# Window attention: the softmax rows scaled inside the transposing product, with a diagonal matrix as its second operand

## The chip, the cores and the metric

The kernel runs on one core of one Trainium2 chip. The metric is the device time of one execution in microseconds. A core has a matrix engine, TensorE (PE in the profile, with its weight loads shown apart as PEld), three engines that work on tiles, VectorE (DVE), ScalarE (ACT) and GpSimd (POOL), and SyncE (SP), whose queue issues most of the DMAs. Each engine runs its own instructions in a fixed order and waits on semaphores for the others. Products of TensorE land in PSUM; GpSimd works on tiles in SBUF only.

## The reference

Two layers work on 512 latent tokens and 256 context tokens of width 1024. Each layer is half a SwiGLU network, a token mixer, and another half SwiGLU network, each closed by a layer norm. The mixer of the second layer ("Mixer 1") is windowed attention with 16 query heads on 4 key heads of 64 columns: a block of 128 queries sees its own block of keys, the block on either side of it within a band, and all 256 context keys, and each head has one extra logit, the sink, which counts in the sum but has no value.

```
s_win  = where(valid, einsum('bqhgd,bkhd->bhgqk', qb, kb), NEG_INF)
s_ctx  = einsum('bqhgd,bkhd->bhgqk', qb, kc)
p = softmax(concatenate([s_win, s_ctx, s_sink], axis=-1))
o = einsum(p[..., :n_win], vb) + einsum(p[..., n_win:n_win + C], vc)
```

## The kernel before

The program is recorded in Python, and a scheduler fixes the order of the instructions on each engine from the dependencies and from its own table of costs; a helper (`behind`) pins a few orders by hand. Tokens lie along the free axis, features along the 128 partitions, and every large product is done in three products of split operands (`mm3`, L166, L168, L169). The weights come through `wunit`: SP loads four raw quarters `wr`, ACT casts each to `wh` (L105), and POOL subtracts to get the rest `wl` (L107). This splitting for later units goes on during the attention, on the same POOL queue that scales the softmax rows.

Mixer 1 is `wa_mixer`. It runs eight units of `attn(s, ...)`, each with two heads h (columns 0 to 63 and 64 to 127 of the partitions), and each over four blocks b of 128 queries. Between the units TensorE has other work: the query projections of a later unit (`wq`), the rotary product (`prq`, L1153), and the output projection of the two units before (`pow`, `wo_pairs`). For one block:

1. `scores` (L888, L889) writes the scores of each head to a PSUM bank, `sw`. Blocks 0 and 3 have two window blocks of keys and fit the context scores behind them, 512 columns. Blocks 1 and 2 have three, 384 columns, and the 256 context scores go to a bank of their own, `sc` (the program calls this `split`).
2. DVE adds the mask and takes the row minimum (L1244, L1247); scores are kept negative, so the minimum stands for the maximum.
3. ACT takes exponentials into SBUF tiles `pw` (L1259) and, for split blocks, `pc` (both heads side by side, L1261), with the row sums `l` and `lc`, and the sink's share `le` (L1263).
4. DVE adds the sums (L1269 or L1272) and takes the reciprocal, 1/l (L1273).
5. POOL multiplies each row of `pw`, and of `pc` for split blocks, by its 1/l in place (`scale_p`, L933).
6. TensorE transposes the tile by blocks of 128 columns against the identity `idn` into a PSUM bank `tpw` or `tpc` (`transpose`, L914). Blocks 0 and 3 have four such products for each head, blocks 1 and 2 have three of `pw` for each head and four of `pc` for both: over the eight units 224 of `pw` and 64 of `pc`.
7. ACT and DVE in turn copy the transposed tile back over the old one (`evac`, L861, L863).
8. TensorE multiplies the transposed tiles with the values `vtw` (`pv_mm`, L924) into the bank `wo`, both heads at a time, 224 and 64 products again. At the end of a unit `split_o` (L929, L930) takes the result out.

The PSUM banks set how far blocks overlap: two banks for `sw`, two for `sc` (shared with other uses), one with tag `t` and two with tag `mm` for the transposes. In the phase's pool, tag `v` has eight tiles of 256 columns in Mixer 1 (`vbufs[0] = 8`, L1135): six for the values, and the rest, with all eight later on, for the normalized inputs `ufl` of the network that follows (L322).

Mixer 0 has its own attention (`na_mixer`) with the same helpers `transpose` and `scale_p`.

## Time and profile before

| | us |
|---|---|
| median of 3 runs | 2696.71 |
| lowest, highest | 2695.93, 2699.86 |
| the profiled execution | 2694.58 |
| its span, first to last instruction | 2692.8 |
| TensorE busy | 2616.0 (97%) |
| VectorE busy | 1810.1 (67%) |
| GpSimd busy | 1676.2 (62%) |
| ScalarE busy | 1198.2 (44%) |
| attention of Mixer 1 in the span | about 2085 to 2305 |

A group row of the profile gives the source line, the engine, the operation, the tiles (out<-in), the shape, how many records there are, then the busy time and the mean duration of one, and then the idle time of the engine just before them with what ended it. A matmul's duration is its latency: the next one starts long before it ends, so the pace of a run of matmuls is read from the starts in the timeline. The chain of waits follows the end of the program back, step by step, to what released each instruction. A releaser such as "POOL pw L933" names the engine, the tile and the line.

### The profile page before, as it was taken

How to read it: one execution, taken by the hardware profiler on the slowest of the kernel's cores; microseconds unless marked ns; L12 is line 12 of the kernel's file. 1: busy time of each engine (PE TensorE's matmuls, PEld its weight loads, DVE VectorE, ACT ScalarE, POOL GpSimd, SP SyncE). 2: the span in 40 equal slices, each digit the busy share in tenths (PEclk: the TensorE clock that was granted, in tenths of full speed). 3: DMA queues.
4: the chain of work that ended last, by engine and by line, in shares of the span. 5: the costliest groups of instructions: out<-in, count | busy, mean ns of one | idle time of the engine just before them, and what ended most of it. 6: DMA issues, size and time to landing. Idle time of an engine off the chain costs nothing.

```text
span 2692.8 us, 47575 instructions
## 1 busy us (share of the span) xinstructions
PE 2616.0 (97%) x16826; PEld 2385.8 (89%) x16826; DVE 1810.1 (67%) x4269; ACT 1198.2 (44%) x2475; POOL 1676.2 (62%) x1523
## 2 busy tenths in 40 slices
PE   8999999999999999999999999999999999899997
PEld 5899999888988899999998899999988777899997
DVE  4977777775445686656565866666668776787765
ACT  5244343266455453443432534434336654544443
POOL 4786767455443566967664678676645544678773
PEclk9999999999999999999999999999999999999999
DMA  9367565523221122454453225546652111243332
GB/s 328 104 180 203 138 163 167 146 70 81 61 57 55 48 74 77 124 132 123 123 135 102 79 78 150 142 133 188 185 152 66 33 32 40 69 117 94 102 92 67
DMA packets 290574, 303.50 MB, mean 113 GB/s; under 512 B 27297, under 2 KB 192417, under 8 KB 289313
## 3 DMA queue, kind: packets, MB, share of 16 engines
q1 hardware_dynamic: 277952, 278.31, 35.1%
q0 software_dynamic: 12096, 22.03, 4.9%
q8 instruction: 133, 2.18, 0.3%
q14 instruction: 105, 0.85, 0.1%
q10 hardware_dynamic: 288, 0.14, 0.0%
HBM read 292.53 MB, written 12.25 MB: 113 GB/s over the span
## 4 chain that ended last, share of the span: by engine, by line
PE 84%; DVE 8%; ACT 3%; issue 2%; DMA 2%; POOL 2%; SPq 0%; POOLq 0%; DVEq 0%; ACTq 0%
PE pd1a L166 2%; PE pd0b L166 2%; PE pd1a L169 2%; PE pd1a L168 2%; PE pd0b L168 2%; PE pd0b L169 2%; PE pd0a L166 2%; PE pd0a L169 2%; PE pd0a L168 2%; PE pd1b L169 1%; PE pd1b L166 1%; PE pd1b L168 1%; DVE z L513 1%; PE wo L924 1%; PE o L924 1%
## 5 line engine op out<-in xcount | busy, mean ns | idle before, releaser
L107 POOL TENSOR_TENSOR wl<-wr,wh 128x512 fp32r<-128x512 f32 x200 | 261.9, 1326 | 163.9 <-ACT wh L105 94.4
L107 POOL TENSOR_TENSOR wl_s<-S,wh_s 128x512 fp32r<-128x512 f32 x240 | 314.3, 1342 | 45.9 <-ACT wh_s L105 29.1
L105 ACT CAST wh_s<-S 128x512 fp32r<-128x512 f32 x256 | 157.2, 621 | 398.7 <-POOL S L655 79.1
L655 POOL TENSOR_TENSOR S<-wr,wr 128x512 f32<-128x512 f32 x128 | 175.3, 1370 | 193.7 <-DMA wr<-in_wst_dram 162.3
L215 DVE CUSTOM_DVE_ANT_0 jk<-wt,cb 128x512 f32<-128x512 f32 x360 | 244.6, 680 | 22.3 <-DMA wt<-in_wmodt_dram 18.2
L107 POOL TENSOR_TENSOR wl_a<-wr,wh_a 128x512 fp32r<-128x512 f32 x144 | 190.7, 1372 | 17.1 <-ACT wh_a L105 13.1
L105 ACT CAST wh_a<-wr 128x512 fp32r<-128x512 f32 x192 | 119.0, 621 | 163.2 <-PE pd1b L168 29.9
L105 ACT CAST wh<-wr 128x512 fp32r<-128x512 f32 x200 | 121.2, 618 | 101.8 <-DMA wr<-in_wst_dram 18.3
L513 DVE SCALAR_TENSOR_TENSOR z<-pd0b,gt,z 128x256 f32<-128x256 f32 (+1 forms) x168 | 96.8, 595 | 43.5 <-PE pd0b L169 43.1
L513 DVE SCALAR_TENSOR_TENSOR z<-pd1a,gt,z 128x512 f32<-128x512 f32 (+1 forms) x150 | 88.2, 605 | 37.3 <-PE pd1a L169 37.1
L513 DVE SCALAR_TENSOR_TENSOR z<-pd0a,gt,z 128x512 f32<-128x512 f32 (+1 forms) x160 | 93.4, 612 | 15.3 <-PE pd0a L169 15.1
L933 POOL TENSOR_SCALAR p<-p,l 128x512 f32<-128x512 f32 x64 | 44.2, 694 | 84.6 <-DVE l L1047 79.8
L655 POOL TENSOR_TENSOR S<-wr,S 128x512 f32<-128x512 f32 x64 | 90.7, 1417 | 2.6
L655 POOL TENSOR_TENSOR S<-S,wr 128x512 f32<-128x512 f32 x64 | 90.6, 1415 | 1.8
L933 POOL TENSOR_SCALAR pw<-pw,l 128x512 f32<-128x512 f32 (+1 forms) x64 | 42.5, 666 | 69.3 <-DVE l L1273 39.7
L343 POOL TENSOR_SCALAR z<-z,ag_None,ab_None 128x256 f32<-128x256 f32 (+1 forms) x69 | 52.1, 759 | 53.3 <-DVE uh L328 34.7
L513 DVE SCALAR_TENSOR_TENSOR z<-pd1b,gt,z 128x512 f32<-128x512 f32 (+1 forms) x91 | 55.1, 622 | 25.3 <-PE pd1b L169 24.8
L1046 ACT ACTIVATE p<-s,m 128x512 f32<-128x512 f32 x64 | 43.8, 687 | 60.5 <-DVE m L1043 57.6
L329 DVE TENSOR_TENSOR ul<-ufl,uh 128x256 fp32r<-128x256 f32 (+1 forms) x88 | 59.1, 676 | 4.2 <-ACT ufl L322 1.9
L322 ACT ACTIVATE ufl<-z,bi_None,sc_None 128x256 f32<-128x256 f32 (+1 forms) x77 | 47.7, 637 | 30.8 <-DVE z L498 30.4
L107 DVE TENSOR_TENSOR wl_a<-wr,wh_a 128x512 fp32r<-128x512 f32 x48 | 58.9, 1236 | 1.6 <-ACT wh_a L105 1.5
L166 PE MATMUL vn<-wh,uh 128*128 128x256 f32 x192 | 54.5, 284 | 0.4 <-DVE nl L882 0.3
(1483 smaller groups left out, 10518.5 us busy)
## 6 DMA issues: line engine op xcount, KB each, us to landing
wr<-in_wst_dram SPq DMA_DIRECT2D x456, 256.0 KB
wt<-in_wmodt_dram SPq DMA_DIRECT2D x206, 256.0 KB
wr_0b<-in_wst_dram SPq DMA_DIRECT2D x47, 256.0 KB
wr_1b<-in_wst_dram SPq DMA_DIRECT2D x47, 256.0 KB
wr_2b<-in_wst_dram SPq DMA_DIRECT2D x47, 256.0 KB
wr_3b<-in_wst_dram SPq DMA_DIRECT2D x47, 256.0 KB
wm<-in_wmod_dram SPq DMA_DIRECT2D x8, 1024.0 KB
zspare<-in_wmodt_dram SPq DMA_DIRECT2D x30, 256.0 KB
```

The source lines that it names most:

```text
L105: nc.scalar.copy(hi[:], src[:])
L107: x = eng.tensor_tensor(out=lo[:], in0=src[:], in1=hi[:].bitcast(F32), op=ALU.subtract)
L166: behind(nc.tensor.matmul(ps, a[0], b[0], start=first, stop=False), in_front[0])
L168: nc.tensor.matmul(ps, a[0], b[1], start=False, stop=False)
L169: last_pe[0] = nc.tensor.matmul(ps, a[1], b[0], start=False, stop=last)
L215: x = nc.vector.tensor_tensor_reduce(out=junk[:], in0=w[:], in1=cb[st], scale=1.0, scalar=0.0, op0=ALU.mult, op1=ALU.add, accum_out=out[st])
L329: return hi, nc.vector.tensor_tensor(out=lo, in0=uv, in1=uo.bitcast(F32), op=ALU.subtract)
L343: nc.gpsimd.tensor_scalar(out=zs, in0=zs, scalar1=prm[2][:, d:d + 1], scalar2=prm[3][:, d:d + 1], op0=ALU.mult, op1=ALU.add)
L513: last[0] = nc.vector.scalar_tensor_tensor(out=zt(d, c0, c1), in0=pd, scalar=gt[:, d, st:st + 1], in1=zt(d, c0, c1), op0=ALU.mult, op1=ALU ...
L655: nc.gpsimd.tensor_tensor(out=t[:], in0=a[:], in1=b[:], op=o)
L924: last_pe[0] = nc.tensor.matmul(po[64 * h:64 * h + 64, :], t[h][0], t[h][1], start=i == 0, stop=i == len(terms) - 1)
L933: nc.gpsimd.tensor_scalar(out=p, in0=p, scalar1=r, scalar2=0.0, op0=ALU.mult, op1=ALU.add)
```

## The change

The row scaling moves from GpSimd into TensorE's transposing product. `transpose` gets a new argument `by`: without it (Mixer 0) it still transposes against the identity, with it each block is an ordinary matrix product of the tile with a diagonal matrix. The product of a tile's transpose with diag(1/l) is the transposed tile with each query's column scaled. `diagonal` makes that matrix on GpSimd, the identity times 1/l, 128 by 128, in one of two buffers with tag `dg`. One diagonal serves all blocks of a head, in `pw` and in `pc`. `vbufs[0]` in Mixer 1 goes from 8 to 7, which makes the room.

```diff
-    def transpose(nm, p, order, tags):
+    def transpose(nm, p, order, tags, by=None):
...
         for j, s in enumerate(order):
-            nc.tensor.transpose(pt[:, j * P:(j + 1) * P], p[:, s * P:(s + 1) * P], idn[:])
+            if by is None:
+                nc.tensor.transpose(pt[:, j * P:(j + 1) * P], p[:, s * P:(s + 1) * P], idn[:])
+            else:
+                nc.tensor.matmul(pt[:, j * P:(j + 1) * P], p[:, s * P:(s + 1) * P], by[s][:], start=True, stop=True)
...
+    def diagonal(nm, r):
+        t = ph["S"].tile([P, P], F32, tag="dg", name=f"dg{nm}", bufs=2)
+        nc.gpsimd.tensor_scalar(out=t[:], in0=idn[:], scalar1=r, scalar2=0.0, op0=ALU.mult, op1=ALU.add)
+        return t
...
-        vbufs[0] = 8
+        vbufs[0] = 7
...
-                es = []
+                es, dg = [], []
...
                     nc.vector.reciprocal(lh, lh)
-                    scale_p(es[h], lh)
-                    if split:
-                        scale_p(ec[:, h * 256:(h + 1) * 256], lh)
-                    transpose(f"w{nm}_{h}", es[h], range(es[h].shape[1] // P), tags)
+                    dg.append(diagonal(f"{nm}_{h}", lh))
+                    transpose(f"w{nm}_{h}", es[h], range(es[h].shape[1] // P), tags, [dg[h]] * 4)
...
                 if split:
-                    transpose(f"c{nm}", ec, range(4), tags)
+                    transpose(f"c{nm}", ec, range(4), tags, [dg[0], dg[0], dg[1], dg[1]])
```

The scheduler orders all engines of the attention anew. Line numbers from L914 on grow by 1 to 8. Tiles are named with the unit, the block and the head: `pw2_1_0` is unit 2, block 1, head 0; `pc2_1` holds both heads of that block; the last number only tells buffers apart.

GpSimd's queue at the beginning of unit 2, before:

```order
L107 TENSOR_TENSOR wl121_0_24594<-wr121_0_24591,wh121_0_24593 128x512
L933 TENSOR_SCALAR pw2_0_1_24049<-pw2_0_1_24049,l2_0_24029 128x512
L107 TENSOR_TENSOR wl121_1_24600<-wr121_1_24597,wh121_1_24599 128x512
L933 TENSOR_SCALAR pw2_1_0_24100<-pw2_1_0_24100,l2_1_24079 128x384
L933 TENSOR_SCALAR pc2_1_24099<-pc2_1_24099,l2_1_24079 128x256
L107 TENSOR_TENSOR wl121_2_24606<-wr121_2_24603,wh121_2_24605 128x512
L933 TENSOR_SCALAR pw2_1_1_24104<-pw2_1_1_24104,l2_1_24079 128x384
L933 TENSOR_SCALAR pc2_1_24099<-pc2_1_24099,l2_1_24079 128x256
L933 TENSOR_SCALAR pw2_2_0_24164<-pw2_2_0_24164,l2_2_24143 128x384
L933 TENSOR_SCALAR pc2_2_24163<-pc2_2_24163,l2_2_24143 128x256
L107 TENSOR_TENSOR wl121_3_24612<-wr121_3_24609,wh121_3_24611 128x512
```

And the same place with the change:

```order
L107 TENSOR_TENSOR wl121_0_24610<-wr121_0_24607,wh121_0_24609 128x512
L940 TENSOR_SCALAR dg2_0_1_24072<-idn_74,l2_0_24037 128x128
L107 TENSOR_TENSOR wl121_1_24616<-wr121_1_24613,wh121_1_24615 128x512
L940 TENSOR_SCALAR dg2_1_0_24120<-idn_74,l2_1_24089 128x128
L107 TENSOR_TENSOR wl121_2_24622<-wr121_2_24619,wh121_2_24621 128x512
L107 TENSOR_TENSOR wl121_3_24628<-wr121_3_24625,wh121_3_24627 128x512
L940 TENSOR_SCALAR dg2_1_1_24129<-idn_74,l2_1_24089 128x128
L940 TENSOR_SCALAR dg2_2_0_24184<-idn_74,l2_2_24153 128x128
```

The four scalings of block 1 have become two diagonals, and that of head 1 now stands behind both `wl121_2` and `wl121_3` instead of behind the first alone. In units 4 and 6 it stands the same way.

TensorE's queue at the end of unit 3, before (`wq2_0` is the query projection that follows; `tpw3_2_0` stands further up):

```order
L924 MATMUL wo3_0_24258<-pw3_1_0_24331,vtw_0_23036 64x128
L914 MATMUL tpc3_2_24421<-idn_74,pc3_2_24394 128x128 x2
L914 MATMUL tpw3_2_1_24416<-idn_74,pw3_2_1_24399 128x128 x3
L914 MATMUL tpc3_2_24421<-idn_74,pc3_2_24394 128x128 x2
L914 MATMUL tpw3_3_0_24464<-idn_74,pw3_3_0_24455 128x128 x4
L166 MATMUL wq2_0_24513<-uh0_101,wh120_0_24491 128x512
```

And with the change:

```order
L927 MATMUL wo3_0_24270<-pw3_1_0_24345,vtw_0_23036 64x128
L917 MATMUL tpw3_2_0_24421<-dg3_2_0_24419,pw3_2_0_24409 128x128 x3
L917 MATMUL tpc3_2_24435<-dg3_2_0_24419,pc3_2_24408 128x128 x2
L917 MATMUL tpc3_2_24435<-dg3_2_1_24428,pc3_2_24408 128x128 x2
L917 MATMUL tpw3_3_0_24479<-dg3_3_0_24477,pw3_3_0_24469 128x128 x4
L166 MATMUL wq2_0_24529<-uh0_101,wh120_0_24507 128x512
```

The number of products is the same; their second operand is now `dg`, whose two buffers alternate. `dg3_3_0` takes the buffer of `dg3_2_0`, so GpSimd can fill it only when the first pair of `tpc3_2` is done, and `tpw3_3_0` stands one pair behind that.

## The prediction

> **What bounds the kernel now.** I read the page first, then the stage by windows, then the chain of waits in it, and last single runs of matmuls in the timeline. The page's busy line says that TensorE carries the whole span:
>
> ```profile
> PE 2616.0 (97%) x16826; PEld 2385.8 (89%) x16826; DVE 1810.1 (67%) x4269; ACT 1198.2 (44%) x2475; POOL 1676.2 (62%) x1523
> ```
>
> An average over the span says little of 220 us of it, so the attention of Mixer 1 is read in windows (columns: busy us and records of PE, PEld, DVE, ACT, POOL, then the granted clock):
>
> ```profile
> 2085.00:2125.00 40.00, 35.31 (x288) 27.93 (x286) 30.55 (x118) 26.66 (x82) 19.61 (x28) 0.96 0.06 14
> 2125.00:2180.00 55.00, 52.79 (x386) 42.01 (x384) 37.28 (x117) 31.32 (x88) 24.06 (x32) 1.00 0.13 34
> 2180.00:2235.00 55.00, 51.23 (x370) 40.29 (x369) 39.36 (x122) 29.61 (x87) 25.66 (x33) 1.00 0.15 39
> 2235.00:2305.00 70.00, 60.15 (x432) 48.12 (x431) 52.20 (x162) 37.96 (x105) 35.89 (x44) 0.98 0.17 46
> sum 220.00, PE 199.49 PEld 158.35 DVE 159.40 ACT 125.55 POOL 105.23; mean PE 49.87 PEld 39.59 DVE 39.85 ACT 31.39 POOL 26.31
> ```
>
> TensorE is busy 91% of these 220 us and GpSimd 48%. In the middle, where projections fill in between units, TensorE stands still for only 2.2 and 3.8 us; at both ends the softmax of a block goes round DVE, ACT and POOL and TensorE waits. What it waits for (longest totals, weight loads and matmuls):
>
> ```profile
> PEld sw L888 <- ACT pw L1259: 14.9, 20, 2.1
> PEld tpw L914 <- POOL pw L933: 6.3, 15, 1.1
> PEld wo L924 <- DVE pw L863: 3.0, 7, 1.1
> PE tpw L914 <- POOL pw L933: 2.4, 6, 0.9
> ```
>
> The wait that ends last is mostly for an exponential to free a score bank. The scaling on POOL, which the change shortens, ends 6.3 us of waiting. The chain through this window, by line, is:
>
> ```profile
> by line: PE wo L924 13.6%; PE tpw L914 6.9%; DVE sw L1244 5.7%; PE sw L888 5.6%; issue 4.8%; PE wq L166 4.2%; PE wq L169 4.2%; PE wq L168 4.1%; ACT pw L1259 4.0%; PE pow L166 3.9%; PE sw L889 3.7%; PE pow L168 3.6%; PE pow L169 3.3%; DVE l
> ```
>
> The transposes themselves are second in it, with 6.9% of 220 us = 15.2 us for `tpw`; POOL's scaling is below the part of the line that the view shows.
>
> **What the change does to TensorE** is the main term. The diff replaces a transpose by a matrix product of two float32 tiles, the same number of times. These rows tell that the two are not the same on the engine:
>
> ```profile
> L914 PE MATMUL tpw<-idn,pw x224: 270/273/476, 2088.5 to 2299.4; 128*128 128x128 f32 x112
> L914 PE MATMUL tpc<-idn,pc x64: 270/273/332, 2094.9 to 2293.7; 128*128 128x128 f32 x64
> L924 PE MATMUL wo<-pw,vtw x448: 272/273/324, 2092.5 to 2301.3; 128*64 128x128 f32 x150
> L924 PE MATMUL wo<-pc,vtw x128: 272/273/324, 2098.1 to 2296.7; 128*64 128x128 f32 x128
> ```
>
> The program has 224 transposes of `pw` and 64 of `pc`, and the trace has one record for each. It has as many products with the values, and the trace has two records for each, 448 and 128: an ordinary float32 product runs as two matmuls, each with its own weight load, a transpose as one. The nearest product in size is the one of the layer norms that spreads a row (`spread`, L407): 128 by 128 against `idn`, float32, exactly the new shape. Beside a run of transposes from the timeline:
>
> ```profile
> 2021.36 1.13 PE L407 MATMUL prl<-idn,yl 128*128 128x128 f32 x8
> 2022.24 0.36 PE L166 MATMUL pd1a_l<-gh1a_l,wh_1b 128*128 128x256 f32 x1
> 2259.46 1.04 PE L914 MATMUL tpw<-idn,pw 128*128 128x128 f32 x8
> 2260.25 0.37 PE L888 MATMUL sc<-wk,wq 128*128 128x256 f32 x1
> ```
>
> Eight records of `prl` are four products (the call over 512 columns makes n // P of them); the next matmul starts 0.88 us after the first, 0.22 us for each product. Eight records of `tpw` are eight products, and the next starts after 0.79 us, 0.099 for each. So each of the 288 products costs about 0.12 us more, **34.6 us** of TensorE time in all.
>
> How much of it lies on the path? The chain holds 15.2 us of `tpw`. `tpc` is below the cut of that line; in proportion of the counts (64 to 224) it adds 4.3, together 19.5 us of 288 x 0.099 = 28.5, about two thirds. The products on the path get 2.2 times as long: 19.5 x 0.22 / 0.099 less 19.5 is +23.8 us if that path stays. Where another engine's wait is as long as the extra 0.3 to 0.5 us of one call, part of it hides; where it is shorter, part of the other third comes on the path. The ends are 0 (all of it in the 20.5 us in which TensorE is idle here, which is less than 34.6, so some 14 would remain even then) and 34.6. I take **+24**.
>
> **What it does to GpSimd.** These go, 96 instructions and 57.9 us:
>
> ```profile
> L933 POOL TENSOR_SCALAR pw<-pw,l 128x512 f32<-128x512 f32 x32 | 23.8, 745 | 30.4 <-DVE l L1273 20.3 <-PE wo L924 4.9 <-ACT wh L105 2.3
> L933 POOL TENSOR_SCALAR pw<-pw,l 128x384 f32<-128x384 f32 x32 | 18.8, 586 | 38.9 <-DVE l L1273 19.4 <-DVE l L1269 10.8 <-DVE l L1272 3.4
> L933 POOL TENSOR_SCALAR pc<-pc,l 128x256 f32<-128x256 f32 x32 | 15.3, 479 | 0.0
> ```
>
> In their place come 64 of 128x128, a shape the trace does not have. From 479 at 256 columns and 586 at 384, each 128 columns cost about 107 ns, so 372 at 128; it is below 479 in any case and, by half of it, above 240. That is 24 us, and 34 us of POOL's work vanish. POOL stood idle half the time, so what counts is the wait that its latency ends: the 6.3 us shrink with 372 against 586 to 745, by a third to a half. In split blocks the second head also no longer stands behind the `pc` of the first. Between 0 and the whole 6.3, I take **-3**.
>
> **The new waits.** A diagonal has two buffers, so the one of a later block waits on POOL until the products that read the buffer are through, and what stands behind it in that queue waits too. The place with the shortest distance is the end of units 3 and 5, where `tpw3_3_0` stands one pair of `tpc3_2` (0.44 us) behind the pair that frees its buffer, while the diagonal takes 0.37 and two hand-overs; some 0.3 us each. In units 2, 4 and 6 the diagonal of head 1 now follows two weight subtractions, of which one more than before is ahead of it:
>
> ```profile
> L107 POOL TENSOR_TENSOR wl<-wr,wh 128x512 fp32r<-128x512 f32 x29 | 37.8, 1308 | 21.7 <-ACT wh L105 19.6 <-PE wq L169 1.8
> ```
>
> That is 1.3 us three times at most, 3.9, if nothing covers it, and TensorE has other products there (the transposes of head 0, eight PV products). Range 0 to 5, I take **+1**.
>
> **What is moved or nearly free.** No DMA is added, and SP's queue keeps its order. POOL frees the raw quarters `wr` by its subtractions, and one such load stands in the chain:
>
> ```profile
> 2260.01 0.67 POOL pw L933
> 2260.68 1.25 POOL wl L107
> 2261.95 3.10 DMA wr<-in_wst_dram
> ```
>
> With 0.37 in place of 0.67 ahead of it the load starts 0.3 earlier; with a subtraction moved ahead of scalings, up to the whole 3.1. I take **-1**. The `v` buffers, seven for eight: the inputs `ufl` that use them are written by ACT in 0.6 us each and read by DVE at once, and DVE waited for one only 1.5 us in all (row below); three free buffers cover that, so nothing, 1.5 if they don't.
>
> ```profile
>   ACT ufl L322: 1.5, 1
> ```
>
> The scheduler's new order of the attention's queues I can only bound: no rule says that it is worse, and with the waits above of 1 or 2 us each, a few more or fewer make 4 us either way; taken as 0.
>
> **Clock.** Two stretches of the attention had a lower granted clock:
>
> ```profile
> 2085.00:2090.00 5.00, 2.72 (x11) 1.56 (x10) 4.09 (x19) 2.79 (x10) 1.37 (x2) 0.85 0.16 42
> 2090.00:2095.00 5.00, 4.93 (x39) 4.35 (x40) 4.00 (x19) 3.72 (x15) 1.95 (x4) 0.81 0.00 0
> 2285.00:2290.00 5.00, 3.21 (x14) 2.92 (x15) 3.39 (x18) 4.35 (x15) 1.69 (x3) 0.66 0.00 0
> ```
>
> 5 x (0.15 + 0.19 + 0.34) = 3.4 us of clock went in these. Both lie where TensorE idles (2.72 and 3.21 busy of 5), which the change does not cure, so 0; a gain of 3.4 at most. The Trainium skill, TensorE: Matmul & The Clock Gate, Part 4: PE-mode transpose, says that transposes do not count as busy for the clock gate. By that rule ordinary products in their place would keep the clock up, and these 3.4 us would come back; the idle in the same rows speaks for the simpler reason.
>
> **Sum.** 24 - 3 + 1 - 1 = **+21 us**. The profiled execution took 2694.58 us (span 2692.8), so 2715.6 beside it; the median of the three runs is 2.1 higher, and by that it is 2717.7. I forecast **2717 us**, 0.8% slower, with 2708 to 2726 as its own range (a third more or less of the main term is 8).
>
> **The rivals.** First, on the other side, **TensorE pays nothing**: the scaled product runs like a transpose, one record, and only POOL's relief counts. That gives -3 to -6.3 for the wait, up to -3.1 for the load: about 2690. For it speaks that a matmul's duration is 273 ns in both kinds of row; against it, that the records are counted double for every float32 product, `prl` among them. 5%. The same skill section puts a transpose at about 275 ns in a kernel's context, and FP8 and Floating Point Precision, section Matmul Precision, a true float32 product at four passes; as an estimate from these pages at 2.4 GHz that is 4 x 128 columns = 213 ns, less than 275, and the change would give back 288 x 0.062 = 18 us, 2679; of the 5% I give it one. The rows differ from the first: transposes start every 0.099 us here, and 273 is only their latency; they agree with the second, at 0.22.
>
> Second, **the waits swallow it**: the extra 0.3 to 0.5 us of a call falls into the 14.9 us of waiting for exponentials, POOL's gains come on top, and the sum is 34.6 - 20.5 - 8, about +6 or less: 2697 to 2705. For it: the ends of the stage are loose, 4.7 and 9.9 us idle. Against it: the transposes are on the path there themselves, ahead of the PV products and of the bank. 14%.
>
> Third, **all of it is exposed, and the new waits too**: 34.6 + 5 - 3, 2733. For it: the middle of the stage has almost no idle time, and the single bank with tag `t` holds back the next transpose longer. Against it: a third of the transposes were off the path. 16%.
>
> **Chances.** The forecast 62%; it pays nothing 5%, the waits swallow it 14%, all exposed 16%; the rest, 3%, is a better order of the queues. The range 2701 to 2733 leaves out the first rival, the lower half of the second and a tail above. A measurement of this kernel can tell about 0.2%, 5.4 us, from no change, so "same" reaches to 2702. Faster 0.05 (the first rival alone), same 0.09 (most of the second), slower 0.86.
>
> **What would show it.** TensorE with 288 records more, 17114, `tpw` with 448 and `tpc` with 128 at a pace of 0.11 us; 64 diagonals on POOL near 372 ns, and POOL's total down by some 34 us; the stage about 241 us long; `tpw` and `tpc` with some 40 us in its chain; little wait behind POOL. Wrong would be a count of 16826, or a stage of unchanged length with the idle time of TensorE gone from its ends.

## The result

The changed kernel took 2715.57 us in the median of 17 runs (2708.79 to 2723.88), the kernel before, in 17 runs beside it, 2700.22. The ratio is 1.0053, 95% interval 1.0041 to 1.0065: **14.3 us slower**, 11 to 17.5. The forecast of 2717 us came close, and part of that is luck: it had 21 us of loss, two thirds of which came, and the kernel before took 3.5 us more in these runs than in the three that the 21 were added to. The single runs of one kernel spread by some 15 us, in part with their granted clock: of the changed kernel's, the seven below 2712 us had 0.995 or 0.996 of it, the ten above 0.992 to 0.996.

The busy line of the page of the profiled execution (2711.55 us, span 2709.7) with the change:

```profile
PE 2643.1 (98%) x17114; PEld 2422.4 (89%) x17114; DVE 1815.7 (67%) x4269; ACT 1199.0 (44%) x2475; POOL 1647.9 (61%) x1491
```

There are 288 more records on TensorE and its busy time is 27.1 us longer, while GpSimd lost 28.3 us and 32 instructions. The four windows of the attention, with the columns of the prediction's fence:

```profile
2085.00:2125.00 40.00, 36.69 (x326) 32.16 (x326) 31.94 (x118) 25.49 (x80) 7.49 (x17) 1.00 0.03 10
2125.00:2180.00 55.00, 54.21 (x421) 46.47 (x421) 33.70 (x112) 30.11 (x85) 17.51 (x25) 1.00 0.14 40
2180.00:2235.00 55.00, 54.72 (x410) 46.12 (x411) 37.52 (x120) 30.47 (x86) 18.68 (x24) 1.00 0.13 39
2235.00:2305.00 70.00, 66.93 (x493) 56.96 (x492) 43.95 (x127) 32.36 (x90) 23.85 (x30) 1.00 0.13 39
```

TensorE is now busy nearly all of the time even in the last window (66.93 of 70, before 60.15), and GpSimd, the fifth busy time of a row, does a half to two thirds of what it did. Equal windows hold different work, though, since the changed kernel is later and later. So from here on the **stage** is measured from the first score product (`sw`) to the first product of the next network (`pa1b`), and read as one window. Before:

```profile
2083.90:2309.00 225.10, 203.56 (x1501) 162.16 (x1499) 163.81 (x530) 128.47 (x368) 109.23 (x140) 0.98 0.14 38
```

With the change:

```profile
2084.90:2325.90 241.00, 229.29 (x1790) 195.82 (x1788) 162.55 (x530) 129.60 (x368) 77.61 (x108) 1.00 0.12 35
```

The stage grew from 225.1 to 241.0 us, by 15.9. (The forecast's 241 was 220 plus 21, in windows that begin later and end earlier; that both read 241 is chance.) Busy time of TensorE grew by 25.7, its idle time fell from 21.5 to 11.7 us, by 9.8; busy and idle time make up the stage, so this is bookkeeping and not yet a cause. What follows the stage is as long as before, 369.6 against 369.4 us to the end of the last matmul. GpSimd did 31.6 us less in the stage; what that was worth is asked below. Every stage length here is read from the one profiled execution of its kernel. The clock in it falls to half in stretches of 3.4 us, which cost up to 1.7 us each: there were two in this stage before and none with the change, so a difference of 2 us between two kernels can be one such stretch.

The groups by tile show what the 288 records are (columns: count, then shortest, median and longest duration in ns, first and last start):

```profile
L917 PEld LDWEIGHTS tpw<-dg,pw x448: 186/192/193, 2089.2 to 2316.2; 128*128 128x128 f32 x150
L917 PE MATMUL tpw<-dg,pw x448: 270/275/377, 2089.4 to 2316.3; 128*128 128x128 f32 x150
L917 PE MATMUL tpc<-dg,pc x128: 270/275/377, 2095.1 to 2310.5; 128*128 128x128 f32 x128
L940 POOL TENSOR_SCALAR dg<-idn,l x64: 367/373/787, 2088.7 to 2312.2; 128x128 f32<-128x128 f32 x64
```

448 for 224 and 128 for 64; the duration of one record hardly moved (275 ns for 273). The pace is in the timeline, at the place that the prediction showed:

```profile
2263.82 1.16 PE L917 MATMUL tpw<-dg,pw 128*128 128x128 f32 x8
2264.74 0.36 PE L888 MATMUL sw<-wk,wq 128*128 128x256 f32 x1
```

Eight records are now four products in 0.92 us, 0.23 for each. The chain through the stage names them first:

```profile
by line: PE tpw L917 19.6%; PE wo L927 14.4%; PE tpc L917 6.2%; PE sw L888 5.4%; PE pow L166 5.3%; PE pow L168 4.9%; PE pow L169 4.7%; PE sw L889 4.6%; PE wq L166 3.8%; PE wq L168 3.8%; PE wq L169 3.8%; DVE sw L1252 2.6%; PE prq L1161 2.0%;
```

25.8% of 241 is 62 us, where `tpw` alone had 15.2 before. All 288 products together take 68.2 us (worked out below), so about nine tenths of them are on the path. And the waits:

```profile
PEld sw L888 <- ACT pw L1267: 4.7, 8, 2.1
PEld tpw L917 <- POOL dg L940: 4.3, 8, 1.3
POOL dg L940 <- DVE l L1281: 30.2, 22, 4.4
POOL dg L940 <- PE tpc L917: 21.0, 6, 4.6
POOL dg L940 <- PE tpw L917: 13.3, 8, 2.9
```

The wait for an exponential to free a score bank fell from 14.9 to 4.7 us: this is most of the idle time that went. TensorE waits 4.3 us for diagonals, where it waited 6.3 for scaled rows. GpSimd waits 34 us for TensorE to release a diagonal's buffer; whether that costs anything is one of the questions below.

### The profile page after: what moved, and what is told of

Read it like the earlier page. It is cut to its first block, busy times and chain, and to the rows that moved or that the text cites. A ratio compares the mean times of both kernels' runs of the same rounds, so it can differ in the third digit from the quotient of the medians.

```text
span 2709.7 us, 48049 instructions
## 1 busy us (share of the span) xinstructions
PE 2643.1 (98%) x17114; PEld 2422.4 (89%) x17114; DVE 1815.7 (67%) x4269; ACT 1199.0 (44%) x2475; POOL 1647.9 (61%) x1491
## 4 chain that ended last, share of the span: by engine, by line
PE 87%; DVE 6%; ACT 2%; POOL 1%; DMA 1%; issue 1%; SPq 0%; POOLq 0%; DVEq 0%; ACTq 0%
PE pd0b L166 2%; PE pd1a L166 2%; PE pd0b L168 2%; PE pd0b L169 2%; PE pd1a L169 2%; PE pd1a L168 2%; PE pd0a L166 2%; PE pd0a L169 2%; PE pd0a L168 2%; PE tpw L917 2%; PE wo L927 1%; PE pd1b L166 1%; PE pd1b L169 1%; PE pd1b L168 1%; PE o L927 1%
## 5 line engine op out<-in xcount | busy, mean ns | idle before, releaser
L107 POOL TENSOR_TENSOR wl_s<-S,wh_s 128x512 fp32r<-128x512 f32 x240 | 320.0, 1363 | 57.4 <-ACT wh_s L105 42.2
L940 POOL TENSOR_SCALAR dg<-idn,l 128x128 f32<-128x128 f32 x64 | 24.9, 390 | 92.5 <-DVE l L1281 30.2
L917 PE MATMUL tpw<-dg,pw 128*128 128x128 f32 x448 | 61.9, 281 | 2.8 <-POOL dg L940 1.1
L917 PEld LDWEIGHTS tpw<-dg,pw 128*128 128x128 f32 x448 | 54.8, 191 | 8.6 <-POOL dg L940 4.3
L322 ACT ACTIVATE ufl<-z,bi_None,sc_None 128x256 f32<-128x256 f32 (+1 forms) x77 | 47.6, 637 | 32.2 <-DVE z L498 31.6
```

What stands on the lines that cost most here:

```text
L107: x = eng.tensor_tensor(out=lo[:], in0=src[:], in1=hi[:].bitcast(F32), op=ALU.subtract)
L322: nc.scalar.activation(uv, zs, AF.Identity, scale=s1, bias=s2)
L917: nc.tensor.matmul(pt[:, j * P:(j + 1) * P], p[:, s * P:(s + 1) * P], by[s][:], start=True, stop=True)
```

## The experiments

The theory (A in the expectations): the second record of an ordinary float32 product is the whole loss, less a few us for GpSimd's shorter link. Its rivals: the two buffers of the diagonal and the new order (B), and a latency of GpSimd that weighs more than 3 us (C).

### The doubled product alone

The kernel before, scaling on GpSimd and all, with Mixer 1's transposes made as ordinary products with the identity:

```diff
-            nc.tensor.transpose(pt[:, j * P:(j + 1) * P], p[:, s * P:(s + 1) * P], idn[:])
+            if plain:
+                nc.tensor.matmul(pt[:, j * P:(j + 1) * P], p[:, s * P:(s + 1) * P], idn[:], start=True, stop=True)
+            else:
+                nc.tensor.transpose(pt[:, j * P:(j + 1) * P], p[:, s * P:(s + 1) * P], idn[:])
...
-                    transpose(f"w{nm}_{h}", es[h], range(es[h].shape[1] // P), tags)
+                    transpose(f"w{nm}_{h}", es[h], range(es[h].shape[1] // P), tags, True)
...
-                    transpose(f"c{nm}", ec, range(4), tags)
+                    transpose(f"c{nm}", ec, range(4), tags, True)
```

> The kernel before, with its transposes in the window attention turned into ordinary float32 products against the same identity; the scaling stays on GpSimd, no diagonals. This is the doubling of TensorE's records alone. Theory A (the loss is the second record of each product): 576 records of tpw and tpc, and 18 to 26 us over the kernel before, so more than the change itself lost (about 14), since nothing comes back from GpSimd. Rival B (the doubling hides in TensorE's waits; the loss comes from the two buffers of the diagonal and from the new order of the queues): 0 to 6 us over the kernel before.

Measured: 2721.39 us, ratio 1.0089 (1.0065 to 1.0113), +24 us (17.5 to 30.5), more than the change itself. The stage as one window, and the group of `tpw`:

```profile
2090.00:2334.90 244.90, 229.96 (x1790) 195.91 (x1788) 167.42 (x530) 128.82 (x368) 109.14 (x140) 1.00 0.12 35
```

```profile
L915 PEld LDWEIGHTS tpw<-idn,pw x448: 186/192/193, 2094.6 to 2325.1; 128*128 128x128 f32 x150
L915 PE MATMUL tpw<-idn,pw x448: 270/275/377, 2094.6 to 2325.2; 128*128 128x128 f32 x150
```

There is no diagonal and no new buffer here, `v` has all its eight tiles, and the loss is there: stage +19.8 us, TensorE busy +26.4, idle -6.6. The doubling alone costs more than the whole change, and the difference of 3.9 us between the two stages, which both lost no clock, is what the diagonals gave back.

### One record with the diagonal's order and buffers

The changed kernel, with the diagonal replaced by a matrix of zeros and ones, so that the product can stay a transpose; GpSimd still writes it from 1/l, but with a comparison in place of the addition. The rows are not scaled (left out).

```diff
-                nc.tensor.matmul(pt[:, j * P:(j + 1) * P], p[:, s * P:(s + 1) * P], by[s][:], start=True, stop=True)
+                nc.tensor.transpose(pt[:, j * P:(j + 1) * P], p[:, s * P:(s + 1) * P], by[s][:])
...
-        nc.gpsimd.tensor_scalar(out=t[:], in0=idn[:], scalar1=r, scalar2=0.0, op0=ALU.mult, op1=ALU.add)
+        nc.gpsimd.tensor_scalar(out=t[:], in0=idn[:], scalar1=r, scalar2=0.0, op0=ALU.mult, op1=ALU.is_gt)
```

> The changed kernel, with the same diagonals made on GpSimd at the same place, of the same shape and with the same two buffers, but filled with ones (1/l greater than 0) so that the product can stay a transpose with one record; the rows of p are not scaled, which is left out. Theory A: 288 records, and faster than the kernel before by 3 to 8 us, which is what the shorter work on GpSimd is worth. Rival B: the waits on the diagonal's buffers and the new order are still there, so 8 to 14 us slower than before.

Measured: 2697.75 us, ratio 0.9998 (0.9984 to 1.0012), no change in the time; the stage, and GpSimd's group:

```profile
2083.80:2303.00 219.20, 200.16 (x1501) 161.02 (x1499) 157.11 (x530) 128.44 (x368) 99.61 (x108) 0.99 0.14 39
```

```profile
L940 POOL TENSOR_SCALAR dg<-idn,l x64: 712/717/1130, 2087.6 to 2291.6; 128x128 f32<-128x128 f32 x64
```

The loss is gone with the second record, although these diagonals took 717 ns each, not 373: the comparison is dearer than the addition, so the test is the harder one for theory A. The stage is 5.9 us shorter than before, with one stretch at half clock instead of two, so up to 1.7 of the 5.9 are clock. What follows it was 5.7 us longer (375.1 against 369.4). TensorE idled 3.9 us more there, 2.1 of them because the next network's first product `pa1b` waited 3.3 us for its input `uh` instead of 1.2, and lost up to 1.7 to one more stretch at half clock. What put the input later was not tested. So the relief of GpSimd shows in its stage and does not reach the end here.

### Four buffers for the diagonal

The changed kernel with `bufs=4` for `dg` and six `v` tiles for seven, which makes the room:

```diff
-        t = ph["S"].tile([P, P], F32, tag="dg", name=f"dg{nm}", bufs=2)
+        t = ph["S"].tile([P, P], F32, tag="dg", name=f"dg{nm}", bufs=4)
...
-        vbufs[0] = 7
+        vbufs[0] = 6
```

> The changed kernel with four buffers for the diagonals instead of two (and six v tiles instead of seven, for the room). GpSimd waited 34 us for products that read a diagonal before it could fill the buffer again. Theory A: these waits lie beside TensorE's own work, so no more than 3 us faster than the changed kernel, 11 to 16 over the kernel before. Rival B: 8 us or more faster than the changed kernel, within 6 of the kernel before.

Measured: 2721.92 us, ratio 1.0086 (1.0061 to 1.0111): no better than with two buffers. The stage, and GpSimd's waits in it:

```profile
2087.80:2329.60 241.80, 229.43 (x1790) 197.07 (x1788) 161.80 (x530) 129.41 (x369) 77.62 (x108) 0.99 0.12 35
```

```profile
POOL dg L940 <- DVE l L1281: 75.6, 45, 6.7
POOL dg L940 <- PE tpc L917: 8.7, 5, 3.8
PEld tpw L917 <- POOL dg L940: 3.3, 5, 1.2
```

GpSimd's 34 us of waiting for a buffer became some 9, and its wait for 1/l grew from 30.2 to 75.6 instead; the stage stayed at 241.8, with one stretch at half clock in it. Rival B's buffers cost nothing that shows. What follows the stage was 6.2 us longer than in the changed kernel (375.8 against 369.6): TensorE idled 3.4 us more there, with the same 3.3 us for `uh` instead of 1.2, and lost up to 1.7 to one more stretch at half clock. What put the input later is open here too.

The same two changes (four diagonals, six `v` tiles) under one record, where TensorE is less full:

```diff
-        t = ph["S"].tile([P, P], F32, tag="dg", name=f"dg{nm}", bufs=2)
-        nc.gpsimd.tensor_scalar(out=t[:], in0=idn[:], scalar1=r, scalar2=0.0, op0=ALU.mult, op1=ALU.add)
+        t = ph["S"].tile([P, P], F32, tag="dg", name=f"dg{nm}", bufs=4)
+        nc.gpsimd.tensor_scalar(out=t[:], in0=idn[:], scalar1=r, scalar2=0.0, op0=ALU.mult, op1=ALU.is_gt)
```

> The one-record diagonal (a transpose by a unit matrix that GpSimd makes from 1/l; rows not scaled) with four buffers of dg and six v tiles. Theory A: stage 218 to 220 us, as with two buffers. Rival B (dg's two buffers hold GpSimd back where TensorE is not doubled): stage 216 or less. Behind the stage the order of the next network decides a few us either way: 384 to 390.

Measured: 2697.31 us, ratio 0.9998 (0.9984 to 1.0013), stage 219.5 us against 219.2 with two. The same answer, with diagonals of 717 ns again.

### What the scaling itself costs

Three kernels took scaling away. The kernel before without any of it (left out, p is not normalised):

```diff
-                    scale_p(es[h], lh)
-                    if split:
-                        scale_p(ec[:, h * 256:(h + 1) * 256], lh)
```

> The kernel before with the scaling of p in the window attention left out altogether: nothing on GpSimd between the reciprocal and the transpose. This is the most that any cheaper scaling can give back. Theory A, from the 6.3 us that weight loads waited for the scaling: 3 to 9 us faster than before. Rival C (GpSimd's latency weighs more than its waits show, since each block's chain runs through it): 12 us or more faster, and then the doubling of the products must cost some 26 or more of the changed kernel's time.

Measured: 2687.9 us, ratio 0.9958 (0.9942 to 0.9973), -9.6 us by the medians and some 11 by the ratio; the stage, 10.7 shorter with as much clock lost as before:

```profile
2094.00:2308.40 214.40, 198.04 (x1502) 162.21 (x1500) 160.37 (x530) 128.19 (x368) 53.09 (x44) 0.98 0.14 40
```

That is all there is to win on this link with transposes of one record. It lies between theory A (3 to 9 us) and rival C (12 or more), and the interval of 7 to 16 us reaches into both; what is shown is that the link weighs more than 3 us there.

The kernel before, with GpSimd scaling only 128 columns of each `pw` (the rest left out), instructions as long as the diagonals:

```diff
-                    scale_p(es[h], lh)
-                    if split:
-                        scale_p(ec[:, h * 256:(h + 1) * 256], lh)
+                    scale_p(es[h][:, 0:P], lh)
```

> The kernel before, in which GpSimd scales only the first 128 columns of each pw and none of pc (the rest of p is left unscaled): 64 GpSimd instructions as long as the diagonals, no new tile, no new buffer, one record per transpose. Theory A: the shorter GpSimd link is worth what the one-record diagonal showed in the stage, 5 to 7 us (stage 218 to 220), the time 2690 to 2693. Rival B (the diagonal's two buffers and the v tile cost something): this stage is shorter than the one-record diagonal's 219.2 by 3 us or more, 216 or less.

Measured: 2690.47 us, ratio 0.9973 (0.9958 to 0.9987), -7.3 us. The group on GpSimd, and the stage:

```profile
L933 POOL TENSOR_SCALAR pw<-pw,l 128x128 f32<-128x128 f32 x64 | 25.6, 401 | 87.0 <-DVE l L1273 39.1 <-DVE l L1269 23.3 <-DVE l L1272 5.1
```

```profile
2085.00:2303.80 218.80, 199.29 (x1501) 161.40 (x1500) 158.91 (x530) 128.49 (x368) 78.26 (x108) 0.99 0.15 39
```

Stage 6.3 us shorter, up to 1.7 of it clock (one stretch instead of two), nearly as with the one-record diagonal (5.9). But these instructions took 401 ns in the mean (376 in the median) and that diagonal 717 in the median, so the gain doesn't follow the length of the instruction. What the two kernels share is one instruction of GpSimd for each head and none for `pc`; no run takes that apart.

And the scaling left out of the kernel with the doubled products (the first experiment's):

> The kernel before with both: Mixer 1's transposes as ordinary float32 products with the unit matrix (two records each), and no scaling of p at all (left out, so p is not normalised). It says what the whole relief of GpSimd is worth under doubled products. Theory A (the second record is the loss, and the scaling is partly hidden behind it): the stage from the first score to the next network's first product is 236 to 241 us, between the 244.9 of doubled products with scaling and the 234 that taking off the whole 10.7 us of the other experiment would leave; the time 2712 to 2717. Rival C (the latency of the scaling is on the path in full, whatever TensorE does): stage 234 us, time 2710 or less. Rival D (TensorE is so full that nothing behind it counts): stage 244 to 245, time as the doubled products alone, 2721.

Measured: 2725.72 us in only four runs, ratio 1.0096 (1.007 to 1.0122), not to be told from the doubled products with scaling, and nearest to rival D. The profiled stage was 3.9 us longer than theirs, 248.8, and this has a reason beside the kernel's own work, in the windows near its end:

```profile
2315.00:2320.00 5.00, 3.40 (x29) 2.86 (x29) 4.23 (x13) 3.04 (x9) 2.71 (x3) 0.77 0.12 24
2320.00:2325.00 5.00, 3.54 (x21) 2.95 (x21) 0.69 (x1) 0.59 (x1) 0.00 (x0) 0.50 0.09 28
2325.00:2330.00 5.00, 4.73 (x26) 4.10 (x22) 1.62 (x9) 1.44 (x3) 0.61 (x1) 0.50 0.01 3
2330.00:2335.00 5.00, 4.69 (x23) 4.69 (x24) 3.95 (x13) 1.26 (x4) 2.98 (x4) 0.53 0.38 105
```

Here 5 x (0.23 + 0.50 + 0.50 + 0.47) = 8.5 us of clock went, and up to 1.7 more near the stage's beginning. Without them the stage would be near 239, in the range of theory A; but that is arithmetic. The median of the runs shows no gain either, but the four runs had less clock, too (0.990 to 0.994 in the mean of a run, against 0.992 to 0.997 in the six of the first experiment). What is shown is that no gain reached the time in these four runs; whether the clock hides one is open.

### Other ways to shorten the link

Two of the one-record experiments, the 128 columns and no scaling at all, say that 7 to 11 us are to be had if GpSimd's link gets shorter and TensorE's products stay transposes. Four kernels tried it with the whole computation.

The scaling moved behind the products with the values: VectorE writes 1/l 64 columns wide, TensorE transposes that once per block, ScalarE copies it, VectorE multiplies a unit's output. Six `v` tiles make room for the new ones.

```diff
-                    nc.vector.reciprocal(lh, lh)
-                    scale_p(es[h], lh)
...
+                    nc.vector.reciprocal(ls[-1][:, 64 * h:64 * h + 64], lh.broadcast_to([P, 64]))
+                if b == bs[-1]:
...
+                    for i, r in enumerate(ls):
+                        nc.tensor.transpose(pr[:, i * P:(i + 1) * P], r[:], idn[:])
+                    rs = t2(f"rw{s}_{b}")[:, 0:len(ls) * P]
+                    nc.scalar.copy(rs, pr[:, 0:len(ls) * P])
...
+            nc.vector.tensor_tensor(out=po[:, c], in0=po[:, c], in1=rs, op=ALU.mult)
             split_o(oh, ol, po[:, c])
```

> A candidate: the rows of p are not scaled at all; instead 1/l is written 64 columns wide by VectorE's reciprocal, transposed once per block by TensorE (32 transposes of one record, 0.1 us each, estimated 3.3 us in all), copied to SBUF by ScalarE once per unit, and VectorE multiplies the summed output with it before the split (10 products over 512 or 256 columns, estimated 0.6 to 0.7 us each). Theory A: no scaling is worth 10.7 us in the stage, the new transposes cost 3 us and the new multiplications at the units' ends 0 to 4: stage 217 to 222 us, time 2690 to 2696. Rival E (the multiplication stands between the last product of a unit and the bank's next use, 10 times 0.7 us in full, and ScalarE's copies too): stage 225 to 230, time 2698 to 2703.

Measured: 2718.42 us, ratio 1.0082 (1.0059 to 1.0105). The reciprocal of the kernel before, then that of this one, and ScalarE's copy, from the groups of the stage:

```profile
L1273 DVE RECIPROCAL l<-l 128x1 f32<-128x1 f32 x64 | 10.1, 159 | 0.9
```

```profile
L1275 DVE RECIPROCAL dg<-l 128x64 f32<-128x64 f32 x64 | 35.2, 550 | 1.1
```

```profile
L1282 ACT COPY rw<-rw 128x512 f32<-128x512 f32 x6 | 3.5, 586 | 15.2 <-PE rw L1280 15.2
L1282 ACT COPY rw<-rw 128x256 f32<-128x256 f32 x4 | 1.5, 372 | 7.6 <-PE rw L1280 7.6
```

The time lies above both expectations, and two costs were missing in them. A reciprocal of 64 columns takes 550 ns, where one of a single column took 159; it stands in VectorE's queue in every block, and 25 us of VectorE's time came with it. And ScalarE waits 22.8 us before its copies, in the queue in which the exponentials stand. The stage was 244.3 us, 19.2 longer than before; about 8.5 of these are clock (0.95 of it was granted). How much of the rest each of the two costs made was not tested.

Part of the scaling moved to ScalarE, to VectorE, or to both. The edit for ScalarE, for VectorE, and for both:

```diff
                     scale_p(es[h], lh)
                     if split:
-                        scale_p(ec[:, h * 256:(h + 1) * 256], lh)
+                        eh = ec[:, h * 256:(h + 1) * 256]
+                        nc.scalar.activation(eh, eh, AF.Copy, scale=lh)
```

```diff
-                    scale_p(es[h], lh)
-                    if split:
-                        scale_p(ec[:, h * 256:(h + 1) * 256], lh)
+                    for e in [es[h]] + ([ec[:, h * 256:(h + 1) * 256]] if split else []):
+                        if h:
+                            nc.vector.tensor_scalar(out=e, in0=e, scalar1=lh, scalar2=0.0, op0=ALU.mult, op1=ALU.add)
+                        else:
+                            scale_p(e, lh)
```

```diff
-                    scale_p(es[h], lh)
+                    if h:
+                        nc.vector.tensor_scalar(out=es[h], in0=es[h], scalar1=lh, scalar2=0.0, op0=ALU.mult, op1=ALU.add)
+                    else:
+                        scale_p(es[h], lh)
                     if split:
-                        scale_p(ec[:, h * 256:(h + 1) * 256], lh)
+                        eh = ec[:, h * 256:(h + 1) * 256]
+                        nc.scalar.activation(eh, eh, AF.Copy, scale=lh)
```

> A candidate: the kernel before, with the scaling of pc's halves (32 instructions of 128x256, 15.3 us of GpSimd in Mixer 1) done by ScalarE; pw stays on GpSimd, one-record transposes. ScalarE's price is near its 128x256 rows, 0.45 us each, 15 us more in Mixer 1 where it is busy 139 of 245. The 128-column scaling showed that 34 us less of GpSimd's scaling shortens the stage by 6.3 us. Theory A (only the length of GpSimd's chain in a block counts, and ScalarE has room): stage 221 to 224 us, time 2694 to 2697. Rival F (ScalarE's new instructions wait for 1/l, with the next block's exponentials queued behind them): stage 226 or more, 2699 or more.

> A candidate: the kernel before, with the scaling of head 1's p (its pw and its half of pc, 48 instructions) done by VectorE and that of head 0 left on GpSimd, so that the two run beside each other. VectorE is busy 181 of 245 us in Mixer 1; the price there is estimated from its 128x512 copies at 0.62 and 128x256 subtractions at 0.43 us, at most 48 times 0.5 = 24 us. Theory A (the length of the link from 1/l to the transposes counts): 29 us less of GpSimd, the stage 219 to 223 us, time 2692 to 2696. Rival G (VectorE, 10 ns of which are on the path for each 100 added, becomes the bound, since its row minima of the next block stand behind): stage 226 or more, 2699 or more.

> A candidate: the kernel before, with pw of head 0 on GpSimd, pw of head 1 on VectorE and both halves of pc on ScalarE. Theory A: GpSimd keeps 32 scalings of 21 us, the longest link of a block is one scaling: stage 217 to 221 us, close to 214.3 of no scaling at all, time 2689 to 2694. Rivals F and G as for the two others: stage 226 or more.

Measured: 2706.17 us for ScalarE (ratio 1.0031, 1.0013 to 1.0048), 2704.23 for VectorE (1.002, 1.0003 to 1.0038), 2708.02 for both (1.0033, 1.0015 to 1.0051). The stages were 4 to 7 us longer than before; by 1.7, 0 and 3.4 us they also lost more clock:

```profile
2096.30:2325.30 229.00, 203.73 (x1501) 163.14 (x1499) 165.56 (x530) 140.61 (x400) 94.74 (x108) 0.98 0.13 37
2099.60:2328.90 229.30, 202.90 (x1501) 162.25 (x1499) 178.85 (x578) 127.81 (x368) 81.04 (x92) 0.99 0.13 37
2090.90:2323.10 232.20, 206.82 (x1502) 164.96 (x1500) 175.76 (x562) 140.26 (x400) 73.43 (x76) 0.97 0.13 37
```

The new instructions on ScalarE in the first and on VectorE in the second:

```profile
L1277 ACT ACTIVATE pc<-pc,l 128x256 f32<-128x256 f32 x32 | 16.3, 511 | 3.3 <-DVE l L1273 3.2
```

```profile
L1276 DVE TENSOR_SCALAR pw<-pw,l 128x512 f32<-128x512 f32 x16 | 9.2, 576 | 0.1
L1276 DVE TENSOR_SCALAR pc<-pc,l 128x256 f32<-128x256 f32 x16 | 8.2, 516 | 0.0
L1276 DVE TENSOR_SCALAR pw<-pw,l 128x384 f32<-128x384 f32 x16 | 7.6, 474 | 0.2
```

The prices were right (16 and 25 us), and GpSimd was relieved of 14 to 36 us in the stage; still each got slower. Every instruction that leaves GpSimd goes into a queue that the next block's exponentials or row minima share, and what TensorE waits for longest in this stage is the exponentials. That wait is longer than the 14.9 us of before in all three, 15.6, 16.7 and, in the third:

```profile
PEld sw L888 <- ACT pw L1259: 17.2, 21, 2.1
```

The stages and times are those that rivals F and G gave; that it is the queues is what the rows suggest, and no run took the queues apart. None of the four beats the kernel before.

### One record with a scaling product

The last run asks whether it is the second record or the scaling that costs. The changed kernel, with p and the diagonal in float32r, whose products in this kernel are one record; both are rounded to it, so the result is less exact. The transposed tile goes to a tile of its own.

```diff
-        t = ph["S"].tile([P, P], F32, tag="dg", name=f"dg{nm}", bufs=2)
+        t = ph["S"].tile([P, P], F32R, tag="dg", name=f"dg{nm}", bufs=2)
...
+        if by:
+            p = t2(f"x{nm}", "sl" if nm[0] == "c" else "t2")[:, :n]
         evac(p[:, :n], pt[:, :n])
...
-                    e = t2(f"pw{nm}_{h}")[:, 0:pw[h].shape[1]]
+                    e = t2(f"pw{nm}_{h}", "t2", F32R)[:, 0:pw[h].shape[1]]
```

> The changed kernel with the two operands of the diagonal product, p and the diagonal, in float32r (p and 1/l are rounded to it, so the result is less exact), its result put in a tile of its own: an ordinary, scaling product in a type whose products in this kernel are one record (the 128x512 products of the projections are). The result's tile needs two more of the six t2 buffers per block. Theory A (it is the number of records that costs): 16826 records, 0.10 to 0.12 us from one product to the next, stage 219 to 224 us, 17 to 22 less than the changed kernel's 240.9, time 2697 to 2704. Rival H (a product that is not a transpose costs more whatever its type): stage 235 or more, time 2712 or more. Between, 226 to 232, it would be the t2 buffers, and the pace of the products says which.

Measured: 2734.42 us, ratio 1.0134 (1.0112 to 1.0155), the slowest of all. The group, the pace of one call in the timeline, and the stage:

```profile
L917 PE MATMUL tpw<-dg,pw x224: 220/275/623, 2087.9 to 2327.9; 128*128 128x128 f32 x112
```

```profile
2188.35 0.56 PE L917 MATMUL tpw<-dg,pw 128*128 128x128 f32 x4
2188.75 0.44 PE L169 MATMUL wq<-uh,wl 128*128 128x512 f32 x1
```

```profile
2083.50:2341.10 257.60, 219.82 (x1502) 183.19 (x1500) 162.89 (x529) 129.75 (x367) 78.19 (x110) 0.91 0.12 33
```

On the question it answers: 224 records, four products in 0.40 us, 0.10 for each. A scaling product of one record keeps the transpose's pace; the second record costs, and not the scaling. Nor is it the longer weight load, which is 191 ns here and 192 with two records (last section). On the time it says nothing: stage and time lie where rival H put them (235 or more, 2712 or more), but its reason, a dearer product, is refuted by the pace. TensorE idled 37.8 us in the stage, and got 0.91 of its clock there, which is up to 24 us. The tile of its own for each result is the edit that I hold responsible, since four `t2` tiles of six are then in use per block; no run separates it from the rest.

## Why the prediction was right, and where not

**The main term, +24.** Its mechanism is shown: the doubled product alone gives +19.8 us in the stage and +24 in the median, and taking the second record away takes the loss away. The step to the number was right only in sum. A call's products cost 0.22 to 0.23 us each as worked out. But I let two thirds of them lie on the path and the rest off it; in the chain of the changed kernel 62 of their 68 us are on it, where the prediction expected some 40. What I had used only for the lower bound counts too: the idle time of TensorE, of which 9.8 us vanished, mostly in the waits for exponentials (14.9 to 4.7). The better account is busy time added, less idle time filled: 25.7 - 9.8 = 15.9.

**Busy time.** 34.6 was expected and 25.7 came. Summed from each start to the next matmul's start or its own end, if that is sooner, `tpw` and `tpc` took 37.4 us before and 68.2 after, +30.8: the calls before ran at more than 0.099 on average, 37.4 / 288 = 0.13. All other products of the stage took some 5 less by the same sum. Up to 3.1 of what went is clock: TensorE was busy for 6.3 us in the two stretches at half clock of the kernel before (rows below), which have no counterpart in the changed one.

**Clock, 0 with 3.4 at most.** In the profiled execution the 3.4 us came back, so the term was at its bound and not at 0. The two stretches of the kernel before, exactly:

```profile
2088.50:2091.90 3.40, 3.27 (x14) 2.77 (x14) 2.59 (x11) 2.88 (x11) 0.69 (x1) 0.50 0.00 0
2286.50:2289.90 3.40, 2.99 (x13) 2.69 (x14) 1.79 (x11) 3.40 (x13) 0.90 (x2) 0.50 0.00 0
```

TensorE was busy in most of both, so the prediction's "both lie where TensorE idles" came from windows of 5 us, which are too wide for it. Over all executions the mean granted clock was 0.9929 to 0.9935 in four sets of the kernel before and 0.9945 in the changed kernel's 17; 0.001 of 2700 us is 2.7, so the times may hold some of this gain as well. Whether the change makes it is open. The Trainium skill, TensorE: Matmul & The Clock Gate, Part 4: PE-mode transpose, says that a transpose does not count as busy in the same way for the clock gate; by that rule ordinary products would keep the clock. The changed kernel and the first experiment, without any loss of clock in the stage, agree; the four-buffer kernel, with a granted clock of 0.99, and the doubled products without scaling, which lost 8.5 us and more among ordinary products, don't. So the rule can't be the whole of it. Idle time can't either: the two kernels that idled most in the stage (0.95 and 0.91 of the clock) lost most, but the one with 8.5 us lost idled 13.5 us, less than the 15.0 of the first experiment's, which lost none; and the same gap of 1.92 us, at the first wait for an exponential, stands 1.4 us ahead of the first stretch in the kernel before and ahead of none in the changed one. What sets it stays open.

**GpSimd's link, -3.** Under-sized. The diagonals took 373 ns each (372 expected). GpSimd's total fell by 28.3 us instead of 34. In the stage the relief was worth 3.9 us with doubled products, and 5.9 and 6.3 with one record, up to 1.7 of each of these two being clock: somewhat more than the 3 of the 6.3 us of waits that I had taken. Without any scaling it is 10.7, more than that row and the 2.4 us of the matmuls beside it. So the rows of waits behind GpSimd were no upper bound. Without scaling, TensorE's wait for an exponential to free a score bank went too, from 14.9 us to

```profile
PEld sw L888 <- ACT pw L1259: 0.6, 3, 0.2
```

while the transposes waited 9.2 us for the exponentials themselves. In the three kernels with transposes of one record and one instruction of GpSimd for each head that wait was 9.6 to 15.4 us, so this is no rule, and no run took the two rows apart.

**New waits, +1.** Nothing. GpSimd waits 34 us for the diagonal's buffers, and two more buffers leave the stage as it was.

**The load, -1, and the tiles of `v`, 0.** A load of `wr` still stands in the chain of the changed kernel, 2.82 us for 3.10, so the -1 isn't there. Six `v` tiles for seven, together with four diagonals, made no difference in the stage; seven for eight was not tried alone.

**The order, 0 within 4 us.** In the stage it can't be told from the rest. What comes behind it can count: with one record the next network gave back 5.7 of 5.9 us won, by a later input and by clock; that the order made the input late is not shown.

In sum: 24 - 3 + 1 - 1 = 21 stood against 19.8 - 3.9 = 15.9 measured in the stage and 14.3 (11 to 17.5) in the time. With the 3.4 us of clock as a term of its own, the stage reads 23.2 - 3.9 - 3.4 = 15.9: by this count the main term was right in size, and most of what the forecast had too much was the clock, which it put at 0. This is arithmetic on one execution of each kernel. "TensorE pays nothing", and the 18 us gained by the prediction's estimate from the Trainium skill, are refuted by the pace; "the waits swallow it" had the right place and took in 9.8 us rather than all 20.5; "all exposed" was right on the chain and wrong on the sum, since idle time was there to be filled.

## What to carry to other kernels

To put a scale into a transposing product is no free ride in float32: the product is then no transpose, runs as two records, and on a full TensorE the second record costs more than a scaling on an engine that is half idle. Price such a trade as busy time added to the bounding engine less the idle time it can fill in that stage, not as a share of the chain that exists before. Before two stages of a few us difference are compared, count the stretches of low clock in each. And a wait that an idle engine ends was not cured, in four kernels here, by giving its work to the engines whose queues the next block needs.

## What was not expected of the hardware

- GpSimd waited 34 us for buffers at no cost that shows; with twice the buffers its wait for 1/l grew from 30.2 to 75.6 us instead.
- A diagonal of the same size took GpSimd 373 ns with a multiplication and an addition, and 717 with a multiplication and a comparison (`is_gt`).
- A reciprocal of 64 columns took VectorE 550 ns, and one of a single column 159.
- The weight load of an ordinary product took 192 ns in the median (the fences above), that of a float32r product with one record 191, and that of a transpose 140, at the same size. The rows are of the kernel before and of the float32r one:

```profile
L914 PEld LDWEIGHTS tpw<-idn,pw x224: 137/140/230, 2088.5 to 2299.3; 128*128 128x128 f32 x112
```

```profile
L917 PEld LDWEIGHTS tpw<-dg,pw x224: 186/191/333, 2087.8 to 2327.8; 128*128 128x128 f32 x112
```

- One kernel lost 8.5 us to a lower clock near the stage's end, with no transpose on TensorE there and 3.4 to 4.7 us of 5 busy. All losses of clock in these stages came in stretches of 3.4 us, or two or more of these on end, at half the clock.
